# Modulation in quarters, a reordered beginning and weight loads in halves, in a hybrid short-convolution and state-space kernel

## The chip, the cores and the metric

The kernel runs on one core of one Trainium2 chip. The metric is the time of one execution on the device in microseconds (us); lower is better. A profiled execution gives the trace from which the rows below are taken, and its times count from the start of its span.

## The reference

One layer of a streaming encoder is applied to a prompt of 2048 tokens and to a sample of 64 tokens, all in float32 with 1024 channels. Cut to what matters here:

```python
mod = c @ w_mod + b_mod                      # w_mod: 1024 x 3072
shift, scale, gate = jnp.split(mod, 3, axis=-1)
h = rmsnorm(x, norm_in_w) * (1 + scale[:, None]) + shift[:, None]
proj = h @ w_in                              # w_in: 1024 x 7184
b_gate, c_gate, h_a, g_a, z, xbc_raw, dt_raw = jnp.split(proj, idx, axis=-1)
# mixer A: y_a = gated_rmsnorm(b_gate * dwconv3(c_gate * h_a), g_a)
# mixer B: chunked state-space scan over dwconv4 + SiLU of xbc_raw, gated by z
out = jnp.concatenate([y_a, y_b], axis=-1) @ w_out
return rmsnorm(x + gate[:, None] * out, norm_f_w)   # and the new conv and scan states
```

So the input projection needs the normalised x, and the shift and scale of all 1024 channels, which come from a product of the conditioning vectors of prompt and sample with the first 2048 columns of w_mod.

## The kernel before, in words

The kernel is written for a manual schedule: every engine works through its own queue in the order of the program, and an instruction waits until its operands are written and its target is free. Engines are called PE (TensorE), ACT (ScalarE), DVE (VectorE), POOL (GpSimd) and SP (which issues all DMAs).

**The projection** is done transposed: h lies in SBUF as channels by tokens, and the product of 128 output columns with 512 tokens is a matmul of a 128 x 128 weight tile with 128 x 512 of h, summed over channels in a PSUM bank. Each operand is split into a high and a low part (`split`: ACT casts, DVE subtracts), and three matmuls (high-high, high-low, low-high) make one product of float32 quality. The first pass takes 1024 tokens, as two halves of 512. Channels and tokens are halved into four blocks of 4 k-tiles of 128 channels each: A11 and A12 are the two channel halves of tokens 0 to 511, A21 and A22 those of tokens 512 to 1023. The work list holds pairs of two times 128 output columns (`work[g]`). From the third pair on (g = 2) the loop at L1226 forms each pair with seven block products (`PRODS`: A11, S1, S2, S4, S3, A12, A22, where S1 to S4 are sums and differences of the blocks) of 12 matmuls each: a Strassen form. The first two pairs are formed plainly with the four blocks and 8 times 12 matmuls each (`plain_product`, L1041), because their blocks come first; S1 to S4 are made meanwhile (`sum_task`, L1092; split at L1021 and L1028). `plain_w` splits a quarter of a pair's weights (L171, L172), `w_hi` and `w_lo` those of the Strassen pairs, `first_w` those of pair 2 in the beginning.

**The beginning**, whose order is written out by hand: x of tokens 0 to 1023 is loaded as eight row tiles of 128 tokens (`load_rows`). ACT squares each and sums (L979), DVE and POOL make the reciprocal root, DVE scales the rows (`x_scale`). PE transposes them, four row tiles to a bank, one bank per k-tile (`turn_first`), and ACT and DVE in turn copy the banks to the stage tiles stA11 to stA22. Banks come from a rotating list, `ring`.

The shift and scale (**modulation**) are made in two halves (`mod_half`). A half is 4 k-tiles of shift and of scale: 2 times 512 columns of w_mod, loaded as eight pieces of 512 KB, each with 2 k-tiles of w_mod's rows and 512 columns (`load_piece`; eight buffers praw). For each of the 8 k-tiles four products of 32 x 256 go to the four 32-row strips of one bank (L917). ACT copies the result (mrow), PE turns it (L923), DVE adds bias and norm weight, and the columns land in bcol (shift) and scol (scale). `block` then applies them to a stage tile's k-tile, ACT casts it to the high part, DVE subtracts for the low part.

SP's order is: x (eight tiles), pieces of half 0 with the nine small parameter rows between them, the weights of pair 0 (`w_load`: one DMA of 1 MB), pieces of half 1, the weights of pair 1, and so on. PE's order is: transposes of x but for the last four k-tiles, parameter rows, half 0, the last transposes, pair 0 with A11 and A21, half 1, pair 1 with A11, pair 0 with A12 and A22, pair 1 with A21, pair 1 with A12 and A22, and then the loop. `w_load(g + 2)` is called in slot 1 of group g, into the buffer that group g leaves.

After the first pass come the second pass (1088 tokens, read back from DRAM), and the mixing phase with the scan and the output projection; the change doesn't touch their code, other than that `w_load` serves all pairs.

Of the kernel before, what the change touches and what calls it, by code (L numbers as in the profile page):

```python
# [8 lines left out]
F32 = mybir.dt.float32  # L9
F32R = mybir.dt.float32r  # L10
# [17 lines left out]
def kernel(  # L28
# [72 lines left out]
    def phase_project():  # L101
# [78 lines left out]
        raws = [hs1.tile([128, KT, 256], F32, tag=f"raw{i}", name=f"raw{i}") for i in range(2)]  # L180
# [40 lines left out]
        def w_load(g):  # L221
            if g >= len(work):
                return
            raw = raws[g % 2] = hs1.tile([128, KT, 256], F32, tag=f"raw{g % 2}", name="raw")
            col = work[g][0]
            SP.dma_start(out=raw, in_=w_in[:, col:col + 256].rearrange("(k p) f -> p k f", p=128))
            wstate[g] = {"raw": raw, "w": {}}
# [679 lines left out]
        def load_piece(g, j):  # L907
            t = mp.tile([128, 2, 512], F32, tag="praw", name="praw", bufs=8)
            SP.dma_start(out=t, in_=w_mod.rearrange("(p k) n -> p k n", k=KT)[:, 2 * j:2 * j + 2, g * 512:(g + 1) * 512])
            return t  # L910

        def mod_half(half, pieces):
            ps = bank()
            for kk in range(KT):
                for j in range(4):
                    raw = pieces[half + 2 * (j // 2)][kk // 2]
                    PE.matmul(ps[32 * j:32 * j + 32, 0:256], cpad[:, kk, :],  # L917
                              raw[:, kk % 2, 256 * (j % 2):256 * (j % 2) + 256], start=(kk == 0), stop=(kk == KT - 1))
            mrow = mp.tile([128, 256], F32, tag="mrow", name="mrow")
            ACT.copy(out=mrow, in_=ps[:, 0:256])  # L920
            pm = bank()
            for i in range(2):
                PE.transpose(pm[:, i * 128:(i + 1) * 128], mrow[:, i * 128:(i + 1) * 128], ident)  # L923
            m = stats.tile([128, 2, 4, 2], F32, tag="mcol", name="mcol", bufs=1)
            for i in range(2):
                DVE.tensor_copy(out=m[:, :, i::2, :],
                                in_=pm[:, i * 128:(i + 1) * 128].rearrange("p (a b q) -> p a b q", a=2, q=32)[:, :, :, 0:2])
            ks = slice(4 * half, 4 * half + 4)
            for a, col in ((0, bcol), (1, scol)):
                bm = ini[:, 64 + 8 * a + 4 * half:68 + 8 * a + 4 * half].unsqueeze(2).to_broadcast([128, 4, 2])  # L930
# [706 lines left out]
```

## Time and profile before

| | us |
|---|---|
| Median of the runs (lowest, highest) | 1771.92 (1771.90, 1772.29) |
| The profiled execution's own time | 1769.35 |
| Its span | 1767.5 |
| PE busy in the span | 1716.4 (97%) |
| DVE busy | 1306.8 (74%) |
| ACT busy | 826.9 (47%) |
| First plain product (L1041) | starts at 34.51 |
| First product of the loop (L276) | starts at 86.00 |

A row of the timeline has the start, the duration, the engine, the line, the operation, what it writes and reads, how many were merged, and in brackets how long the engine was idle before it and what ended that. PEld is PE's loading of the stationary operand, which overlaps its matmuls. A product of two float32 operands (not split) is recorded as two matmuls. A row of the windows has the stretch, its length, and for each engine the busy time and the number of instructions; then the granted clock of PE as a share of the full one, the busy share of the DMA engines, and GB/s. In the chain in order of time a row is the start, the duration and what the chain passed through.

### The profile page before, as it was taken

The page shows a single profiled execution, that of the slowest core. Times are in us where ns is not written, and L with a number is a line of the kernel's source. Part 1 is how long each engine was busy: PE and PEld are TensorE (multiplying, and loading weights), DVE is VectorE, ACT ScalarE, POOL GpSimd, SP SyncE. Part 2 cuts the span into 40 slices and gives each one's busy share as a digit, 9 for nine tenths or more (in the row PEclk, how much of TensorE's full clock was granted, in tenths as well). Part 3 has the DMA queues.
Part 4 walks back from the last instruction along what each step waited for, and adds up shares of the span by engine and source line. Part 5 has one row for each costly group of instructions (what it writes and reads, how often), then busy time and mean ns, then how long its engine had stood idle before and what let it go on. Part 6 is the DMA issues. An engine that isn't in the chain of part 4 may idle for free.

```text
span 1767.5 us, 26974 instructions
## 1 busy us (share of the span) xinstructions
PE 1716.4 (97%) x10561; PEld 1512.3 (86%) x10561; DVE 1306.8 (74%) x2019; ACT 826.9 (47%) x1575; POOL 102.5 (6%) x224
## 2 busy tenths in 40 slices
PE   5999999999999999999999999999899999999997
PEld 4788888887887799999999999999588888888886
DVE  5787779766576646678768767646788888888885
ACT  5644344444653645434333443325455555545551
POOL 0000000000000000001001000000011111101011
PEclk9999999999999999999999999999899999999999
DMA  9222323232548742322322242324653343434341
GB/s 338 72 76 92 96 84 102 89 107 86 170 151 287 248 123 61 91 74 76 113 82 73 74 119 79 113 90 143 213 179 139 137 150 125 160 107 169 108 149 36
DMA packets 186722, 220.20 MB, mean 125 GB/s; under 512 B 21300, under 2 KB 152356, under 8 KB 186596
## 3 DMA queue, kind: packets, MB, share of 16 engines
q1 hardware_dynamic: 186596, 218.49, 38.2%
q8 instruction: 83, 1.36, 0.3%
q14 instruction: 43, 0.35, 0.1%
HBM read 164.31 MB, written 54.15 MB: 124 GB/s over the span
## 4 chain that ended last, share of the span: by engine, by line
PE 86%; DVE 5%; DMA 4%; ACT 3%; issue 2%; SPq 0%; POOL 0%; POOLq 0%; DVEq 0%; ACTq 0%
PE bank L276 54%; PE mm L1430 14%; PE mm L1437 7%; PE sd L1355 2%; PE sd L1359 2%; PE sd L1361 2%; PE sd L1327 1%; DMA h_q<-hs_d 1%; PE sd L1331 1%; DMA praw<-in_w_mod_dram 1%; PE bank L1041 1%; DVE w L233 1%; DMA hq_d<-h_q 0%; DMA xt<-in_x_prompt_dram 0%; PE bank L530 0%
## 5 line engine op out<-in xcount | busy, mean ns | idle before, releaser
L276 PE MATMUL bank<-hiS,w 128*128 128x272 f32 (+1 forms) x2560 | 598.8, 323 | 9.6 <-ACT keep L301 9.5
L276 PEld LDWEIGHTS bank<-hiS,w 128*128 128x128 f32 x2560 | 432.4, 189 | 46.4 <-ACT keep L301 13.0
L276 PE MATMUL bank<-hiA,w 128*128 128x272 f32 (+1 forms) x1920 | 448.9, 322 | 5.8 <-DVE z_row L309 2.4
L276 PE MATMUL bank<-loS,w 128*128 128x272 f32 (+1 forms) x1280 | 412.4, 322 | 0.0
L276 PEld LDWEIGHTS bank<-hiA,w 128*128 128x128 f32 x1920 | 322.8, 188 | 34.7 <-DVE z_row L309 3.3
L233 DVE TENSOR_TENSOR w<-raw,w 128x512 fp32r<-128x512 f32 x318 | 217.9, 688 | 160.0 <-ACT w L242 149.0
L242 ACT CAST w<-raw 128x512 fp32r<-128x512 f32 x318 | 196.1, 622 | 256.7 <-PE bank L276 131.2
L276 PE MATMUL bank<-loA,w 128*128 128x272 f32 (+1 forms) x960 | 308.2, 321 | 0.0
L276 PEld LDWEIGHTS bank<-loS,w 128*128 128x128 f32 x1280 | 242.2, 189 | 15.8
L276 PEld LDWEIGHTS bank<-loA,w 128*128 128x128 f32 x960 | 180.5, 188 | 11.9
L301 ACT COPY keep<-bank 128x272 f32<-128x272 f32 (+1 forms) x240 | 105.9, 450 | 130.7 <-PE bank L276 130.2
L382 DVE SCALAR_TENSOR_TENSOR acc<-raw_row,par,acc 128x1024 f32<-128x1024 f32 (+1 forms) x96 | 126.5, 1318 | 2.0
L233 DVE TENSOR_TENSOR raw<-raw 128x512 f32<-128x512 f32 x161 | 111.0, 690 | 3.7
L1430 PE MATMUL mm<-woh,vbh 128*128 128x512 f32 (+1 forms) x272 | 110.0, 404 | 0.0
L1430 PE MATMUL mm<-woh,vah 128*128 128x512 f32 (+1 forms) x272 | 109.4, 402 | 0.0
L1430 PE MATMUL mm<-wol,vbh 128*128 128x512 f32 (+1 forms) x272 | 106.6, 392 | 0.0
L1430 PE MATMUL mm<-wol,vah 128*128 128x512 f32 (+1 forms) x272 | 106.4, 391 | 0.0
L1289 ACT ACTIVATE lt<-rb,acum 128x128 f32<-128x128 f32 x240 | 73.4, 388 | 3.5 <-DMA rb<-r_d 3.1
L242 ACT CAST w<-t 128x512 fp32r<-128x512 f32 x53 | 32.8, 618 | 74.1 <-PE bank L276 74.1
L1437 PE MATMUL mm<-woh,vbh 128*128 128x512 f32 (+1 forms) x272 | 67.2, 389 | 0.0
L1437 PE MATMUL mm<-woh,vah 128*128 128x512 f32 (+1 forms) x272 | 67.2, 389 | 0.0
L1455 ACT ACTIVATE t<-xr 128x512 f32<-128x512 f32 (+1 forms) x34 | 21.5, 633 | 92.9 <-DVE xr L1454 92.9
(282 smaller groups left out, 2381.8 us busy)
## 6 DMA issues: line engine op xcount, KB each, us to landing
raw<-in_w_in_dram SPq DMA_DIRECT2D x56, 1024.0 KB
xb_d<-acc SPq DMA_DIRECT2D x32, 512.0 KB
xb<-xb_d SPq DMA_DIRECT2D x32, 512.0 KB
rb<-r_d SPq DMA_DIRECT2D x30, 512.0 KB
xt<-in_x_prompt_dram SPq DMA_DIRECT2D x16, 512.0 KB
praw<-in_w_mod_dram SPq DMA_DIRECT2D x16, 512.0 KB
z_d<-z_row SPq DMA_DIRECT2D x16, 512.0 KB
va_d<-c_row SPq DMA_DIRECT2D x16, 512.0 KB
```

The source lines that it names most:

```text
L233: DVE.tensor_tensor(out=out, in0=a, in1=b, op=ALU.subtract)
L242: ACT.copy(out=w[:, 0], in_=w_src(g, j))
L276: PE.matmul(ps[:, 0:n], w[:, a, k, :], h[:, k, o:o + n], start=(s in (0, 1, 5) and k == 0 and i == 0), stop=(k == 3 and i == 2), skip_grou ...
L301: ACT.copy(out=keep[s][:, o:o + n], in_=b["y" if s == 1 else "x"][:, 0:n])
L382: DVE.scalar_tensor_tensor(out=acc[:, 0:n], in0=r[:, k:k + n], scalar=cb_w(k, t), in1=acc[:, 0:n], op0=ALU.mult, op1=ALU.add)
L1289: ACT.activation(out=lt[:, h, :], in_=rb[:, h, :], func=AF.Relu, scale=-1.0, bias=acum[:, c, h0 + h:h0 + h + 1])
L1355: PE.matmul(py4[64 * e:64 * e + 64, j, :], xd[:, 2 * j + e, :], lt[:, 2 * j + e, :], start=True, stop=True)
L1359: PE.matmul(po4[:, j, :], state[:, hf, j * 128:(j + 1) * 128], xb[:, 6 + j // 2, :], start=True, stop=True)
L1361: PE.matmul(ps[:, g * 256:(g + 1) * 256], bc[:, g, :], xe[:, 4 * g:4 * g + 4, :].rearrange("p h q -> p (h q)"), start=True, stop=True)
L1430: PE.matmul(ps[:n], hl[:, 0, k, 0:n], wo[k0 + k][i][:, nn * 512:(nn + 1) * 512], start=(k == 0 and i == 0), stop=False)
L1437: PE.matmul(ps[:n], hl[:, 1, k, 0:n], wo[k0 + k][0][:, nn * 512:(nn + 1) * 512], start=False, stop=(k == 7))
L1455: ACT.activation(out=t[:n], in_=xr[:n, s], func=AF.Square, accum_out=ss[:n, nn:nn + 1])
```

## The change

- **Modulation in quarters.** A quarter is 2 k-tiles of shift and scale. It needs four pieces of 512 KB, each now 4 k-tiles of w_mod's rows by 256 columns. `mod_half` becomes `mod_mm` (32 products of 32 x 128 to four strips of a bank, and the copy to mrow) and `mod_turn` (one transpose; DVE reads it in PSUM directly, without the copy mcol). The two are called with other work between them for quarters 0 and 1, and directly one behind the other for quarters 2 and 3.
- **Loads.** First x of tokens 0 to 511, quarter 0 with the small rows, half of pair 0's weights (k-tiles 0 to 3), quarter 1, x of tokens 512 to 1023, half of pair 1's weights, the other half of pair 0's; quarter 2, quarter 3, the other half of pair 1's.
- **Order of work.** Pair 0 takes A11's k-tiles 0 and 1 after quarter 0, and 2 and 3 after quarter 1. The squares, the scaling and the transposes of tokens 512 to 1023 come between products. Of a half's four row tiles one is scaled on ACT (`scale_first`). Pair 1 with A11 and pair 0 with A21 come ahead of quarters 2 and 3, and pair 1 with A21 right behind them. S3 is made ahead of quarters 2 and 3, into rows 6 and 7; A21's parts lie in rows 0 to 3.
- **Weights.** `w_load` issues two DMAs of 512 KB for every pair, also in the loop.

```diff
-        def w_load(g):
+        def w_load(g, parts=(0, 1)):
             if g >= len(work):
                 return
-            raw = raws[g % 2] = hs1.tile([128, KT, 256], F32, tag=f"raw{g % 2}", name="raw")
+            if 0 in parts:
+                wstate[g] = {"raw": hs1.tile([128, KT, 256], F32, tag=f"raw{g % 2}", name="raw"), "w": {}}
             col = work[g][0]
-            SP.dma_start(out=raw, in_=w_in[:, col:col + 256].rearrange("(k p) f -> p k f", p=128))
-            wstate[g] = {"raw": raw, "w": {}}
+            for i in parts:
+                SP.dma_start(out=wstate[g]["raw"][:, 4 * i:4 * i + 4, :], in_=w_in[512 * i:512 * i + 512, col:col + 256].rearrange("(k p) f -> p k f", p=128))
...
-        def load_piece(g, j):
-            t = mp.tile([128, 2, 512], F32, tag="praw", name="praw", bufs=8)
-            SP.dma_start(out=t, in_=w_mod.rearrange("(p k) n -> p k n", k=KT)[:, 2 * j:2 * j + 2, g * 512:(g + 1) * 512])
+        def load_piece(q, j):
+            t = mp.tile([128, 4, 256], F32, tag="praw", name="praw", bufs=8)
+            k0, col = 4 * (j // 2), (j % 2) * D + q * 256
+            SP.dma_start(out=t, in_=w_mod.rearrange("(p k) n -> p k n", k=KT)[:, k0:k0 + 4, col:col + 256])
             return t
...
-        def mod_half(half, pieces):
+        def mod_mm(q):
+
             ps = bank()
             for kk in range(KT):
                 for j in range(4):
-                    raw = pieces[half + 2 * (j // 2)][kk // 2]
-                    PE.matmul(ps[32 * j:32 * j + 32, 0:256], cpad[:, kk, :],
-                              raw[:, kk % 2, 256 * (j % 2):256 * (j % 2) + 256], start=(kk == 0), stop=(kk == KT - 1))
-            mrow = mp.tile([128, 256], F32, tag="mrow", name="mrow")
-            ACT.copy(out=mrow, in_=ps[:, 0:256])
+                    raw = pieces[q][2 * (kk // 4) + j // 2]
+                    PE.matmul(ps[32 * j:32 * j + 32, 0:128], cpad[:, kk, :],
+                              raw[:, kk % 4, 128 * (j % 2):128 * (j % 2) + 128], start=(kk == 0), stop=(kk == KT - 1))
+            mrow = mp.tile([128, 128], F32, tag="mrow", name="mrow", bufs=2)
+            ACT.copy(out=mrow, in_=ps[:, 0:128])
+            return mrow
+
+        def mod_turn(q, mrow):
             pm = bank()
-            for i in range(2):
-                PE.transpose(pm[:, i * 128:(i + 1) * 128], mrow[:, i * 128:(i + 1) * 128], ident)
-            m = stats.tile([128, 2, 4, 2], F32, tag="mcol", name="mcol", bufs=1)
-            for i in range(2):
-                DVE.tensor_copy(out=m[:, :, i::2, :],
-                                in_=pm[:, i * 128:(i + 1) * 128].rearrange("p (a b q) -> p a b q", a=2, q=32)[:, :, :, 0:2])
-            ks = slice(4 * half, 4 * half + 4)
+            PE.transpose(pm[:, 0:128], mrow, ident)
+            m = pm[:, 0:128].rearrange("p (a e q) -> p a e q", a=2, q=32)
+            ks = slice(2 * q, 2 * q + 2)
             for a, col in ((0, bcol), (1, scol)):
-                bm = ini[:, 64 + 8 * a + 4 * half:68 + 8 * a + 4 * half].unsqueeze(2).to_broadcast([128, 4, 2])
-                DVE.tensor_tensor(out=col[:, ks, :], in0=m[:, a], in1=bm, op=ALU.add)
-            nin = par[:, 120 + 4 * half:124 + 4 * half].unsqueeze(2).to_broadcast([128, 4, 2])
+                bm = ini[:, 64 + 8 * a + 2 * q:66 + 8 * a + 2 * q].unsqueeze(2).to_broadcast([128, 2, 2])
+                DVE.tensor_tensor(out=col[:, ks, :], in0=m[:, a, :, 0:2], in1=bm, op=ALU.add)
+            nin = par[:, 120 + 2 * q:122 + 2 * q].unsqueeze(2).to_broadcast([128, 2, 2])
...
-        first = [load_rows(range(4), range(4)), load_rows(range(4, 8), range(4, 8))]
+        first = [load_rows(range(4), range(4))]
         load_mods(0)
-        w_load(0)
+        w_load(0, (0,))
+        load_mods(1)
+        first.append(load_rows(range(4, 8), range(4, 8)))
+        w_load(1, (0,))
+        w_load(0, (1,))
...
-        pairs_ss = []
-        for h, xs in enumerate(first):
-            ss = x_ss()
-            for i, (off, n, t) in enumerate(xs):
-                ACT.activation(out=stage["A22"][:, 2 * (i % 2):2 * (i % 2) + 2, :].rearrange("p k t -> p (k t)"), in_=t,
-                               func=AF.Square, accum_out=ss[:, i, 0:1])
-            pairs_ss.append(ss)
-            if h == 0:
-                x_scale(xs, ss, True)
-        turn_first(0, range(4))
-        x_scale(first[1], pairs_ss[1], True)
-        turn_first(0, range(4, 8))
-        turn_first(1, range(4))
+        def square_first(h, i):
+            off, n, t = first[h][i]
+            ACT.activation(out=stage["A22"][:, 2 * (i % 2):2 * (i % 2) + 2, :].rearrange("p k t -> p (k t)"), in_=t,
+                           func=AF.Square, accum_out=first_ss[h][:, i, 0:1])
+
+        def scale_first(h):
+            ms = stats.tile([128, 4], F32, tag="ms4", name="ms4", bufs=2)
+            DVE.tensor_scalar(out=ms, in0=first_ss[h][:, :, 0], scalar1=1.0 / D, scalar2=EPS, op0=ALU.mult, op1=ALU.add)
+            POOL.tensor_tensor(out=ms, in0=ms, in1=mhalf.to_broadcast([128, 4]), op=ALU.pow)
+            for i, (off, n, t) in enumerate(first[h]):
+                if i == 0:
+                    ACT.activation(out=t, in_=t, func=AF.Copy, scale=ms[:, 0:1])
+                else:
+                    DVE.tensor_scalar(out=t, in0=t, scalar1=ms[:, i:i + 1], scalar2=None, op0=ALU.mult)
+
+        first_ss = [x_ss() for _ in range(2)]
+        for i in range(4):
+            square_first(0, i)
+        scale_first(0)
         pt = bank()
         PE.transpose(pt[:, 0:128], rows, ident)
         PE.transpose(pt[:, 128:208], irow, ident[0:80, 0:80])
         DVE.tensor_copy(out=par, in_=pt[:, 0:128])
         DVE.tensor_copy(out=ini, in_=pt[:, 128:208])
+        mrow = mod_mm(0)
+        turn_first(0, range(2))
+        mod_turn(0, mrow)
...
-        mod_half(0, pieces)
-        ring[:] = [4, 5, 6, 7]
-        turn_first(1, range(4, 8))
-        load_mods(1)
-        w_load(1)
         for q in ("A11", "A12", "A22"):
             h_tile(q, 512)
-        rows21 = [[row(4 + 2 * n + i, [128, 2, 512], "a21", F32R) for i in range(2)] for n in range(2)]
         plain_w(0, 0)
-        run([block("A11", k, DVE) for k in range(4)])
+        run([block("A11", k, DVE) for k in range(2)])
         drain()
         plain_w(0, 1)
         for j in range(2):
-            plain_product(0, "A11", j)
+            plain_product(0, "A11", j, range(2))
+        ring[:] = [2, 3, 6, 7]
+        turn_first(0, range(2, 4))
+        mrow = mod_mm(1)
+        turn_first(0, range(4, 6))
+        mod_turn(1, mrow)
+        square_first(1, 0)
+        turn_first(0, range(6, 8))
+        load_mods(2)
+        rows21 = [[row(2 * n + i, [128, 2, 512], "a21", F32R) for i in range(2)] for n in range(2)]
+        run([block("A11", k, DVE) for k in range(2, 4)])
+        drain()
+        for j in range(2):
+            plain_product(0, "A11", j, range(2, 4))
+        for i in range(1, 4):
+            square_first(1, i)
+        plain_w(1, 0)
+        scale_first(1)
+        plain_w(1, 1)
+        plain_product(1, "A11", 0)
+        turn_first(1, range(4))
+        load_mods(3)
+        w_load(1, (1,))
+        plain_product(1, "A11", 1)
         run([block("A21", k, (ACT, DVE)[k % 2]) for k in range(4)])
         drain()
+        turn_first(1, range(4, 8))
         for j in range(2):
             plain_product(0, "A21", j)
+        ring[:] = [6, 7]
         plain_w(0, 2)
         plain_w(0, 3)
         w_load(2)
-        mod_half(1, pieces)
+        S3 = [row(6 + i, [128, 2, 512], "stS3") for i in range(2)]
+        for k in range(4):
+            DVE.tensor_tensor(out=S3[k // 2][:, k % 2, :], in0=stage["A11"][:, k, :], in1=stage["A21"][:, k, :], op=ALU.subtract)
+        for q in (2, 3):
+            mrow = mod_mm(q)
+            mod_turn(q, mrow)
         mods.close()
         for q in ("S1", "S2"):
             home[q] = home.get("S1") or pool(hstack, "hs2", bufs=1, side="right", reuse_waits="tile")
         for q in ("S2", "S1"):
             h_tile(q, 544)
-        plain_w(1, 0)
-        plain_w(1, 1)
-        plain_w(1, 2)
         for j in range(2):
-            plain_product(1, "A11", j)
+            plain_product(1, "A21", j)
+        ring[:] = [4, 5, 6, 7]
         run([block(q, k, (ACT, DVE)[k % 2]) for q in ("A12", "A22") for k in range(4)])
         drain()
         work[0][1]["begin"](0)
         S = [row(2 + i, [128, 2, 512], "stS") for i in range(2)]
...
             if n == 2:
                 drain()
+                plain_w(1, 2)
                 plain_w(1, 3)
                 w_load(3)
...
-        for j in range(2):
-            plain_product(1, "A21", j)
         first_w(1)
         for k in range(4):
             sum_task("S4", k)[0]()
         work[1][1]["begin"](0)
-        S3 = [row(6 + i, [128, 2, 512], "stS3") for i in range(2)]
-        for k in range(4):
-            sum_task("S3", k)[0]()
```

More of the change, by code (lines that the diff above doesn't have):

```diff
@@ L179, in phase_project @@
             row(i, [128, 1094], f"row{i}_")
-        raws = [hs1.tile([128, KT, 256], F32, tag=f"raw{i}", name=f"raw{i}") for i in range(2)]
+        for i in range(2):
+            hs1.tile([128, KT, 256], F32, tag=f"raw{i}", name=f"raw{i}")
         def load_rows(chunks, rows):
@@ L944, in phase_project, with load_mods @@
         small.append((irow[64:80, :], tile_rows(b_mod)[0:16, :]))
-        def load_mods(half):
+        def load_mods(q):
             for j in range(4):
-                for g in (half, half + 2):
-                    pieces[g][j] = load_piece(g, j)
-                    for _ in range(min(2, len(small))):
-                        dst, src = small.pop(0)
-                        SP.dma_start(out=dst, in_=src)
+                pieces[q][j] = load_piece(q, j)
+                for _ in range(min(3, len(small))):
+                    dst, src = small.pop(0)
+                    SP.dma_start(out=dst, in_=src)
         ring[:] = list(range(8))
@@ L1028, in drain, with plain_product @@
                 DVE.tensor_tensor(out=lo, in0=t, in1=hi.bitcast(F32), op=ALU.subtract)
-        def plain_product(g, q, j):
+        def plain_product(g, q, j, ks=range(4)):
             i, f = j // 2, j % 2
             c = 2 * (q in ("A21", "A22")) + f
-            if i == 0:
+            if i == 0 and ks[0] == 0:
                 plain[g]["ps", c] = bank(4 * g + c)
@@ L1037, in plain_product @@
             w = plain[g][j]
-            for k in range(4):
+            for k in ks:
                 hi, lo = (x[k // 2][:, k % 2, :] for x in rows21) if q == "A21" else (x[:, k, :] for x in hq[q])
@@ L1084, in sum_task @@
         def sum_task(q, k):
-            t = (S3 if q == "S3" else S)[k // 2][:, k % 2, :]
+            t = S[k // 2][:, k % 2, :]
             a, b, op = {"S1": (stage["A21"][:, k, :], stage["A22"][:, k, :], ALU.add),
                         "S2": (t, stage["A11"][:, k, :], ALU.subtract),
-                        "S4": (stage["A12"][:, k, :], t, ALU.subtract),
-                        "S3": (stage["A11"][:, k, :], stage["A21"][:, k, :], ALU.subtract)}[q]
+                        "S4": (stage["A12"][:, k, :], t, ALU.subtract)}[q]
             def step():
@@ L1123, in phase_project @@
         work[1][1]["begin"](0)
-        S3 = [row(6 + i, [128, 2, 512], "stS3") for i in range(2)]
-        for k in range(4):
-            sum_task("S3", k)[0]()
         stg_stack.close()
```

## The prediction

> **What bounds the kernel now.** I read the page first (shares of the engines, the chain's shares), then the chain in order of time for the first 110 us, then that stretch's timeline and its windows; the rest of the span only for what the halved weight loads touch. All times are us of the profiled execution.
>
> ```profile
> span 1767.5 us, 26974 instructions
> PE 1716.4 (97%) x10561; PEld 1512.3 (86%) x10561; DVE 1306.8 (74%) x2019; ACT 826.9 (47%) x1575; POOL 102.5 (6%) x224
> PE 86%; DVE 5%; DMA 4%; ACT 3%; issue 2%; SPq 0%; POOL 0%; POOLq 0%; DVEq 0%; ACTq 0%
> ...
> 20.01 7.67 DMA praw<-in_w_mod_dram
> ...
> 34.51 13.12 PE bank L1041 x48
> ...
> 92.51 310.61 PE bank L276 x1368
> ```
>
> TensorE is busy for 97% of the span, and from 92.51 on it runs 311 us without a wait. What the beginning loses before that point is lost for the whole kernel. So the question is one number: when does the steady stretch begin, 92.51 now? Until 27.7 the chain is loads of x and of modulation weights; the first product is at 34.51. What lies between them and 92.51:
>
> ```profile
> 23.74 3.25 PE L917 MATMUL bank<-praw,cpad 128*32 128x256 f32 x52
> ...
> 27.72 1.06 PE L917 MATMUL bank<-praw,cpad 128*32 128x256 f32 x12 [0.74 <-DMA praw<-in_w_mod_dram]
> ...
> 47.56 3.66 PE L917 MATMUL bank<-praw,cpad 128*32 128x256 f32 x64
> ...
> 52.74 0.17 DVE L933 SCALAR_TENSOR_TENSOR scol<-scol,par 128x8 f32<-128x8 f32 x1
> 52.83 1.89 DVE L172 TENSOR_TENSOR w<-raw,w 128x512 fp32r<-128x512 f32 x3
> ...
> 86.00 0.39 PE L276 MATMUL bank<-hiA,w 128*128 128x512 f32 x1
> ...
> 92.51 0.50 PE L276 MATMUL bank<-hiS,w 128*128 128x512 f32 x1 [0.90 <-ACT keep L301]
> 52.20:69.60 17.40, 16.77 (x73) 13.59 (x74) 16.54 (x32) 13.68 (x23) 0.00 (x0) 1.00 0.00 0
> 75.30:95.00 19.70, 18.80 (x83) 15.23 (x83) 16.83 (x28) 12.31 (x23) 0.20 (x2) 1.00 0.23 65
> ```
>
> The last modulation columns (scol) are ready at 52.9. From there two chains run side by side: TensorE's, which reaches the first group of the loop at 86.00, and the one of VectorE and ScalarE (splits of A12, A22, S1 to S4 and the weights), which ends later: the wait before 92.51 is for ScalarE's copy, and the windows show VectorE at 16.54 of 17.40 and 16.83 of 19.70. So **the last modulation plus 39.6 us of vector work (52.9 to 92.5)** sets the start, not the first product.
>
> **The change, part by part.** Durations that the sum uses, all of before:
>
> ```profile
> 15.07 6.58 PE L214 MATMUL bank<-cst,xt 128*128 128x128 f32 x32 [0.19 <-DVE xt L209]
> 29.52 1.91 PE L214 MATMUL bank<-cst,xt 128*128 128x128 f32 x16
> 35.83 1.05 PE L1041 MATMUL bank<-hiA,w 128*128 128x512 f32 x2
> 41.91 5.72 PE L1041 MATMUL bank<-a,w 128*128 128x512 f32 x24
> 11.22 1.02 POOL L207 TENSOR_TENSOR ms<-ms,mhalf 128x4 f32<-128x4 f32 x1 [10.00 <-DVE ms L206]
> 12.28 2.74 DVE L209 TENSOR_SCALAR xt<-xt,ms 128x1024 f32<-128x1024 f32 x4 [1.21 <-POOL ms L207]
> L979 ACT ACTIVATE stA<-xt x8: 1056/1056/1059, 5.9 to 14.8; 128x1024 f32<-128x1024 f32 x8
> 21.85 2.48 DVE L973 COPY stA<-bank 128x512 f32<-128x512 f32 x4
> 38.63 1.17 ACT L1021 CAST a<-stA 128x512 fp32r<-128x512 f32 x2
> 37.78 0.81 ACT L1009 ACTIVATE stA<-stA,bcol,scol 128x512 f32<-128x512 f32 x1
> 41.20 1.29 DVE L1028 TENSOR_TENSOR a<-stA,a 128x512 fp32r<-128x512 f32 x2 [0.17 <-ACT a L1021]
> 51.29 0.37 ACT L920 COPY mrow<-bank 128x256 f32<-128x256 f32 x1 [8.56 <-PE bank L917]
> 80.87 2.49 DVE L1092 TENSOR_TENSOR stS<-stA,stA 128x512 f32<-128x512 f32 x4
> 32.00:33.00 1.00, 0.00 (x0) 0.00 (x0) 0.34 (x1) 0.63 (x2) 0.00 (x0) 1.00 1.05 389
> ```
>
> That gives, in a queue: a product matmul 0.228 (0.43 at half clock), a transpose 0.11 (0.2 in the stretch before 21), a square with its readout 1.28, a 512-wide cast 0.52, a subtraction or evacuation on VectorE 0.60, the scaling of a row 0.66.
>
> *Loads.* The same bytes, in another order: the first quarter (four pieces of 512 KB) stands behind half of x. Before, 8 pieces and all of x landed at 27.7; now 4.2 MB less stand ahead. At the 387 GB/s of the windows below that is 10.8 us less. Pieces with 1 KB rows run a little slower: the weights alone, in such rows, moved 376 and 364, which adds 0.05 to 0.1 a piece. The first quarter is in at 17 to 18, the second at about 25, the last at about 45 (estimates by these rates). The new SP issues are few; SP is nowhere on the chain here.
>
> ```profile
> 35.00:36.00 1.00, 1.00 (x3) 0.67 (x3) 1.00 (x3) 0.32 (x1) 0.00 (x0) 0.50 1.05 387
> 73.00:74.00 1.00, 1.00 (x6) 0.78 (x5) 0.69 (x2) 0.98 (x2) 0.00 (x0) 1.00 1.07 376
> 74.00:75.00 1.00, 1.00 (x6) 0.83 (x5) 0.96 (x3) 0.99 (x2) 0.00 (x0) 1.00 1.06 364
> 1067.61 0.68 PE L711 MATMUL bank<-smp,smp 64*64 64x64 f32 x16
> 1251.57 1.09 PE L1355 MATMUL sd<-lt,xd 128*64 128x128 f32 x16
> ```
>
> *Modulation.* A half was 64 recorded matmuls of 256 columns in 3.66; a quarter is 64 of 128. Half as long each, 1.83, if the columns set the pace; 3.66 if the number does. The nearest rows of narrower matmuls on column tiles: 16 of 64 columns take 0.68, the last one's own 0.22 off: 0.03 each; 16 of 128 columns on two tiles 0.054, which is 0.027 on four. I take 1.83 and keep 3.66 for the range. The Trainium skill has a rule against this edit: its page "TensorE: Matmul & The Clock Gate", section "Wait — 56ns, not 53.3ns?", puts the sequencer at about 62 ns a matmul when its hardware decode is off, which would make a quarter 4.0. The row of 0.03 disagrees.
>
> *The order of the queues.* I walked the five queues in the new order with these durations, each instruction starting when its engine and its operands are free:
>
> 1. First quarter in at 17.4, its remaining matmuls at half clock to 19.4; eight transposes (1.65) to 20.7; transposed row and three short VectorE operations: first scol 21.6.
> 2. Weight subtraction 0.60, block 0.5, cast 0.6: first product at **23.9** (34.5 before). TensorE idled over 3 us, so I take half clock here: 12 products to 28.6 (2.7 at full clock).
> 3. Eight transposes 0.9, second quarter 1.83 (its data long in), eight transposes 0.9: 32.2; second scol 33.0. ScalarE now has an evacuation, a square of the second half of x (1.28) and another evacuation before the cast of A11's third block: cast done 35.3, TensorE idle 2.5. Products to 38.5.
> 4. ScalarE: the cast of the fourth block, three squares 3.84 (35.7 to 39.5), then the weight cast for pair 1: 40.1. TensorE waits 1.9 for it, products to 43.2.
> 5. VectorE is queued behind that weight cast: its subtraction to 40.8, mean 0.2, POOL 1.02, scaling 42.0 to 44.1 (one of four rows now on ScalarE, 1.06, which saves VectorE 0.66 a half). Sixteen transposes 1.8 to 45.6; evacuations to 46.5.
> 6. A21's four blocks: 4.7 (as 37.8 to 42.5 before), to 50.9; the evacuations of x's last quarter behind them (1.2) free bank 2 for A21's products at 51.5. 24 products 5.5: 57.0.
> 7. Only then come quarters three and four, one behind the other: 1.83, copy and transpose 0.6, twice, last scol at **62.5** (61.2 with full clock in step 2). Their data were in 12 us before.
>
> So the second half of x, which in the kernel before is squared, scaled and three quarters turned while loads hold everybody up, now passes through the in-order queues between products, and the last modulation moves from 52.9 to 62.5: 9.6 later. In exchange the vector chain behind it is shorter: S3's four subtractions (2.4) now stand ahead of it, and of three weight subtractions two have gone ahead (1.2): 39.6 - 3.6 = 36.0. The wait in the first loop group ends at 62.5 + 36.0 = 98.5, against 92.5: **+6.0**. TensorE itself reaches that group at about 89.5 instead of 86.0 and then idles about 3.
>
> *Clock.* The rows at 32 to 33 (no TensorE work) and 35 to 36 (clock 0.50) show it halved after an idle stretch of 3 us. The same page, Part 1, has a free-running window of about 3.4 us whose idleness halves the rate; by that rule step 2 and perhaps the wait before 98.5 run at half speed, and where the window falls differs from run to run; the trace agrees. With full clock in step 2 the sum is +4.7; with half clock also after the last wait it is +7.7. I take half clock in step 2 alone.
>
> *Half loads in the loop.* 54 pairs get one more issue.
>
> ```profile
> SPq L226 <- DVE w L233: 267.8, 45, 18.7
> 70.56 0.37 SPq L226 DMA_DIRECT2D raw<-in_w_in_dram  x1
> ```
>
> SP waits for the buffer, not for its own pace, and a group's load is issued a group (84 matmuls of 0.228, 19 us) ahead of its use; the one issued at 70.56 was still moving at 74 to 75 (rows above) and hardly longer. Cost: nothing, with that cover; without it 0.37 per load at one or two places where stores queue behind it (520 to 630), so 0 to +1.
>
> **The sum:** 1767.5 + 6.0 = 1773.5 of span. The execution itself took 1769.35, the median of the runs is 1771.92; against the median: **1778**.
>
> **The rivals.**
> - *TensorE alone sets the start (faster).* From 23.9 on it owes 192 products (43.7), three quarters (5.5), 56 transposes (6.2) and the slow clock (2): 81.3, where 86.0 stood: -4.7, 1767. For it speaks that TensorE was 97% busy and that the data would allow the last modulation at 47.5. It needs the last scol before 92.5 - 36.0 = 56.5; that is the point which decides. Against it: step 6 would have to lose 6 us of waits.
> - *No change beyond 3.5 us.* Full clock throughout and a middle that overlaps 1 to 2 us better than my queues: +1 to +3.5, 1774.
> - *Small matmuls cost by number.* At 0.057 each, a quarter 3.66: +1.8 four times, +13, 1785; against it the 0.03 above. This is where the page's 62 ns would end.
> - *The change doesn't do what it says:* if the first weight split waits for the whole pair's weights, the first product stays at 35, and everything behind it comes 11 later than forecast: +17, 1789. Against such a coarse wait speaks that TensorE began on A11's first block before the fourth was cast:
>
> ```profile
> 34.51 0.73 PE L1041 MATMUL bank<-hiA,w 128*128 128x512 f32 x1 [3.08 <-ACT hiA L1021]
> 36.74 0.62 ACT L1021 CAST hiA<-stA 128x512 fp32r<-128x512 f32 x1 [0.44 <-DVE stA L1011]
> ```
>
>
> **How the numbers follow.** Within 0.2% (3.5 us) a measurement of this kernel can't tell from no change. Forecast (+3.5 to +10): 0.64. TensorE alone: 0.12. No change: 0.14. By number 0.05, coarse wait 0.05. Slower 0.74, same 0.14, faster 0.12. The likeliest case's own range is 1775.5 to 1782 (clock and loop terms, -1 for the walk). To leave out no more than two in ten the range takes in the no-change case and half of the faster one's distance below, and the by-number case above: 1770.5 to 1785.
>
> **What would show it.** First product near 24; 64 recorded modulation matmuls in 1.8; TensorE idle 2 to 3 us before A11's third block, 2 before pair 1, 1.5 before A21; the last scol at 61 to 63, 9 us after the last modulation piece has landed 12 us earlier; at the first loop group a wait for ScalarE's copy three times as long as the 0.90 now; everything behind shifted alike. A last scol before 57 makes the forecast wrong, and so does a vector chain behind it that is not near 36.

## The result, and the profile after

Slower, by more than forecast: 1789.41 us median (1788.56 to 1791.19) against 1771.91, ratio 1.01 with a 95% interval of 1.0084 to 1.0116. That is +17.5 where +6 was forecast; the direction was right, and the time lies above the range. It is close to the 1789 of the rival with the coarse wait, but by chance: that rival had the first product at 35, and it came at 25.35.

The page of the changed kernel, and five pieces of its chain in order of time (start, length, what, matmuls in a row):

```profile
span 1786.4 us, 27300 instructions
PE 1726.6 (97%) x10689; PEld 1516.3 (85%) x10689; DVE 1306.6 (73%) x2019; ACT 828.7 (46%) x1579; POOL 101.8 (6%) x224
PE 84%; DVE 5%; ACT 4%; DMA 4%; issue 2%; SPq 0%; POOL 0%; POOLq 0%; DVEq 0%; ACTq 0%
```

```profile
13.12 3.51 DMA irow<-in_b_mod_dram
17.13 3.57 PE bank L921 x64
25.35 4.75 PE bank L1056 x12
52.35 5.81 PE bank L1056 x24
101.69 316.02 PE bank L278 x1368
```

TensorE's share is the same 97%, and its busy time is 10.2 us longer (the 128 matmuls more are the modulation's, each half as long). The steady stretch starts at 101.69 (92.51 before), and its first 1368 matmuls take 316.02 (310.61). The rest, from 417.71 to the end, takes 1368.7; before, from 403.12, it took 1364.4. So the span's 18.9 us are 9.2 of a later start, 5.4 in that stretch, and 4.3 behind it.

The start. Timeline rows of TensorE (lines 921, 1056, 278) and VectorE (936, the last step of scol; 994, the scaling of x's second half); in brackets the idle time and what ended it:

```profile
17.06 3.64 PE L921 MATMUL bank<-praw,cpad 128*32 128x128 f32 x64
22.73 0.16 DVE L936 SCALAR_TENSOR_TENSOR scol<-scol,par 128x4 f32<-128x4 f32 x1
25.35 0.80 PE L1056 MATMUL bank<-hiA,w 128*128 128x512 f32 x1 [2.92 <-ACT hiA L1036]
30.90 1.96 PE L921 MATMUL bank<-praw,cpad 128*32 128x128 f32 x64
34.34 0.16 DVE L936 SCALAR_TENSOR_TENSOR scol<-scol,par 128x4 f32<-128x4 f32 x1
36.59 0.50 PE L1056 MATMUL bank<-hiA,w 128*128 128x512 f32 x1 [1.71 <-ACT hiA L1036]
40.09 0.60 ACT L171 CAST w<-raw 128x512 fp32r<-128x512 f32 x1
42.63 2.08 DVE L994 TENSOR_SCALAR xt<-xt,ms 128x1024 f32<-128x1024 f32 x3 [1.13 <-POOL ms L989]
52.35 5.81 PE L1056 MATMUL bank<-a,w 128*128 128x512 f32 x24 [1.44 <-ACT w L171]
63.66 0.16 DVE L936 SCALAR_TENSOR_TENSOR scol<-scol,par 128x4 f32<-128x4 f32 x1
90.94 0.39 PE L278 MATMUL bank<-hiA,w 128*128 128x512 f32 x1
101.69 0.80 PE L278 MATMUL bank<-hiS,w 128*128 128x512 f32 x1 [5.10 <-ACT keep L303]
```

The first product came forward from 34.5 to 25.35, and a quarter took 1.96 (the first one 3.64). But the last scol was ready at 63.8 instead of 52.9, and the wait for ScalarE's copy in the first loop group grew from 0.90 to 5.10. Behind it the clock was halved, in the windows' column behind POOL:

```profile
102.00:103.00 1.00, 1.00 (x3) 0.81 (x3) 0.81 (x2) 0.64 (x2) 0.00 (x0) 0.50 0.06 4
106.00:107.00 1.00, 1.00 (x4) 0.71 (x4) 0.24 (x1) 0.00 (x0) 0.00 (x0) 0.50 0.38 118
107.00:108.00 1.00, 1.00 (x5) 0.86 (x4) 0.00 (x0) 0.78 (x2) 0.00 (x0) 0.89 0.00 0
```

Neither explains the later matmuls. The prediction wanted "everything behind shifted alike"; but with the clock full again a loop matmul follows the one before it after 228.9 ns on average, before after 226.9 (starts in the trace, 512 columns).

### The profile page after: what moved, and what is told of

Same layout as the page of the kernel before. It is cut to its first block, busy times and chain, and to the rows that moved or that the text cites. A ratio compares the mean times of both kernels' runs of the same rounds, so it can differ in the third digit from the quotient of the medians.

```text
span 1786.4 us, 27300 instructions
## 1 busy us (share of the span) xinstructions
PE 1726.6 (97%) x10689; PEld 1516.3 (85%) x10689; DVE 1306.6 (73%) x2019; ACT 828.7 (46%) x1579; POOL 101.8 (6%) x224
## 4 chain that ended last, share of the span: by engine, by line
PE 84%; DVE 5%; ACT 4%; DMA 4%; issue 2%; SPq 0%; POOL 0%; POOLq 0%; DVEq 0%; ACTq 0%
PE bank L278 54%; PE mm L1462 13%; PE mm L1469 6%; PE sd L1391 2%; PE sd L1387 2%; PE sd L1393 2%; DMA h_q<-hs_d 1%; DMA wo_raw<-in_w_out_dram 1%; PE sd L1359 1%; PE sd L1363 1%; DVE w L235 1%; PE bank L1056 1%; PE bank L921 1%; ACT w L244 0%; PE bank L532 0%
## 5 line engine op out<-in xcount | busy, mean ns | idle before, releaser
L278 PE MATMUL bank<-hiS,w 128*128 128x272 f32 (+1 forms) x2560 | 603.3, 325 | 13.3 <-ACT keep L303 13.2
```

The lines of the kernel that those rows point to most:

```text
L278: PE.matmul(ps[:, 0:n], w[:, a, k, :], h[:, k, o:o + n], start=(s in (0, 1, 5) and k == 0 and i == 0), stop=(k == 3 and i == 2), skip_grou ...
```

## Experiments on the pace of the matmuls

The change takes one thing away that no step of the prediction looked at: the tile mcol, 64 bytes of each partition in the stats pool. Everything that is allocated behind it moves down by 64 bytes, the loop's weight tiles among it: the compiled program places w0 at byte 31008 instead of 31072. The moving tiles, at the other end of SBUF, stay. (The end with the low addresses is called the left side below.) Rival reasons were the halved loads in the loop, and the chance of one execution.

**The 64 bytes put back** in the changed kernel:

```diff
 ks = slice(2 * q, 2 * q + 2)
+stats.tile([128, 2, 4, 2], F32, tag="mcol", name="mcol", bufs=1)
```

> The changed kernel with a 64-byte tile that nothing reads put back into the stats pool where before had mcol, so that the weight tiles of the loop (w0 at 31072 bytes, as before, not 31008) lie where they lay before. Address theory (the place of the weight tiles sets the pace of the loop's matmuls): mean distance of loop matmuls in the first pass back from 228.9 to 226.7 ns, the drift of about 7 us behind the first groups gone, about 1782.5. Half-load theory (two 512 KB loads per pair instead of one of 1 MB disturb TensorE) and chance-of-the-execution theory: no change, 1788 to 1791, distance 228.9 ns.

Measured: 1782.09 (1781.38 to 1783.98), 7.3 less than the change; against before 1.0063 (1.0051 to 1.0076). The mean distance is back at 226.9 ns. Its chain still has the late start, and a short stretch at half clock:

```profile
101.57 312.20 PE bank L278 x1368
```

**The 64 bytes taken away** from the kernel before (mcol from the pool mp):

```diff
-m = stats.tile([128, 2, 4, 2], F32, tag="mcol", name="mcol", bufs=1)
+m = mp.tile([128, 2, 4, 2], F32, tag="mcol", name="mcol", bufs=1)
```

> The kernel before with mcol's 64 bytes taken from the pool mp instead of stats, nothing else: the weight tiles lie 64 bytes lower, as in the changed kernel. Address theory: distance of loop matmuls in the first pass 228.9 instead of 226.7 ns and about 1778 to 1779 (before: 1772). The other theories: 1772, distance 226.7 ns.

Measured: 1777.65, ratio 1.0043 (1.0031 to 1.0056): +6.4 with not one instruction changed. Its chain:

```profile
92.55 313.47 PE bank L276 x1368
```

Same start as before to 0.04 us, 229.1 ns a matmul instead of 227.1 (310.61 / 1368).

**Whole loads again** in the changed kernel (one transfer of 1 MB from the third pair on):

```diff
+if g >= 2:
+    SP.dma_start(out=wstate[g]["raw"], in_=w_in[:, col:col + 256].rearrange("(k p) f -> p k f", p=128))
+    return
 for i in parts:
```

> The changed kernel with the weights of every pair from the third on loaded by one transfer of 1 MB again; the halves remain for the first two pairs. Half-load theory: the drift of about 7 us goes, about 1782, distance of loop matmuls 226.7 ns. Address theory: no change, 1788 to 1791, 228.9 ns.

Measured: 1790.22 (1786.62 to 1795.69), mean distance 229.0 ns. The pace, which that theory was to change, stayed, so it falls; a cost of the halved loads below a few us can't be seen beside this spread.

**Which tiles, and which places.** Eight more copies of the kernel before, each with one unused tile more (or mcol moved) and nothing else changed. First other amounts in the stats pool:

> The kernel before with 32 bytes more in the stats pool: the weight tiles start 32 bytes higher (w0 at 31104, a multiple of 128 minus 0, instead of 31072). If what counts is whether a tile starts at 96 bytes or 32 bytes past a multiple of 128 because the moving tiles start at 96 (equal offsets are good), the pace gets slower than 226.7 ns and the time rises by 3 to 8 us, 1775 to 1780. If the multiple itself counts (start on a 128-byte line is good): 226.7 ns or less, at most 1772.

> The kernel before with 32 bytes less in the stats pool (w0 at 31040, 64 bytes past a multiple of 128; before 96 past it with 226.9 ns a matmul, the changed kernel 32 past with 228.9, and 0 past with 233.3 and 1792.8 us). Theory that the place within 128 bytes decides and 96 is the one good place: 228 to 234 ns, 1776 to 1793. Theory that only a start on a 64-byte line or the like is bad: 233 ns, 1793. If neither, 226.9 ns and 1771.

> The kernel before with 128 bytes more in the stats pool (w0 at 31200, 96 past a multiple of 128 as before). Theory that the place within 128 bytes decides: 226.9 ns and 1771, no change. Theory that the absolute address, or the distance of the weights to the moving tiles, decides: another pace, 228 to 234 ns, and 5 to 22 us more.

> The kernel before with 256 bytes more in the stats pool. Theory of a period of 256 bytes in the distance of weights to moving tiles: 226.9 ns and 1771. Theory of no period so short: 228 to 234 ns, 1776 to 1793, as with 128 bytes (232.5 ns, 1790.5).

> The kernel before with 64 bytes more in the stats pool. Theory that odd multiples of 32 bytes are the bad ones (233.3 ns at -32 and 32) and even ones mild (228.9 at -64): about 229 ns and 1777. Theory that every other place is as bad as 32: 233 ns, 1790.

| left side moved by (bytes) | us, median | ratio (95%) | chain: length, matmuls | ns each |
|---|---|---|---|---|
| 0 (before) | 1771 | 1 | 310.61, 1368 | 227.1 |
| -64 | 1777.65 | 1.0043 (1.0031 to 1.0056) | 313.47, 1368 | 229.1 |
| -32 | 1793.07 | 1.0128 (1.0107 to 1.0149) | 325.04, 1392 | 233.5 |
| 32 | 1792.80 | 1.0121 (1.0104 to 1.0138) | 325.05, 1392 | 233.5 |
| 64 | 1792.66 | 1.0113 (1.0096 to 1.013) | 319.47, 1368 | 233.5 |
| 128 | 1790.53 | 1.0109 (1.0092 to 1.0126) | 318.17, 1368 | 232.6 |
| 256 | 1771.05 | 0.9999 (0.9989 to 1.0008) | 310.61, 1368 | 227.1 |

My first rules (a place within 128 bytes, a start on some line) fell with 32, 64 and 128. What 256 bytes more leave is exactly what was there before:

```profile
92.34 310.61 PE bank L276 x1368
```

Then only t3 and the kept sums, then the weights and what lies behind them:

> The kernel before with a 32-byte tile in the pool lp between the weight tiles and t3: only t3, the kept sums and junk lie 32 bytes higher; weights, rows and moving tiles stay. Theory that the weights' place sets the pace: 226.9 ns and 1771. Theory that the places of the kept sums or t3 do (ScalarE and VectorE write there while TensorE runs): 228 to 234 ns, 1776 to 1793.

> The kernel before with the 32-byte tile in lp ahead of the weight tiles: w0 to w6 and what lies behind them 32 bytes higher; the rows, the carries and everything of the later phases stay. Theory that the weights' place sets the pace: 233.3 ns as in the run with 32 bytes more in the stats pool, and 13 us more from the loop alone, about 1785 (that run had 1792.8, 8 us of it behind the loop, where other tiles had moved too). Theory of the rows: 226.9 ns and 1771.

The first: 1771.37, ratio 0.9998 (0.9989 to 1.0008). The second: 1784.23, 1.0062 (1.0046 to 1.0078), and

```profile
88.80 325.03 PE bank L276 x1392
```

233.5 ns, as with the whole side moved. So it is the weights. The 8.6 us between 1784.23 and 1792.8 are of later phases, whose tiles moved only in the other run. The traces tell which: the output projection. Its loaded tiles vah and vbh lie on the left side, its moving tiles (woh, wol) do not. One of its groups of 256 matmuls (busy time, mean ns of one, which overlaps the next), first with only the weights of the loop moved, then with the whole side moved by 32:

```profile
L1438 PE MATMUL mm<-woh,vah 128*128 128x512 f32 x256 | 63.2, 389 | 0.0
```

```profile
L1438 PE MATMUL mm<-woh,vah 128*128 128x512 f32 x256 | 64.9, 395 | 0.0
```

On average its matmuls follow each other after 227.6 and 233.1 ns, which makes about 9 us over its 1632 matmuls of 512 columns; from the first product of the mixing phase to the end the two runs took 523.4 and 531.8.

Last, the weights left alone, and the hi and lo tiles of the four sums moved down by 32 bytes:

> The kernel before with a 32-byte tile in the pool of the moving tiles, by which the hi and lo tiles of the four sums lie 32 bytes lower; those of the blocks and all weights stay. Theory that the distance of the weights to the moving tiles sets the pace: the products with sums (four of seven) at another distance, 228 to 234 ns, those with blocks 226.9 as before; 4 to 9 us more. Theory that the weights' own place sets it: 226.9 ns for all and 1771.

Measured: 1778.94, ratio 1.0035 (1.0025 to 1.0046). One loop group of its timeline:

```profile
148.32 0.40 PE L277 MATMUL bank<-hiS,w 128*128 128x512 f32 x1
...
159.52 0.39 PE L277 MATMUL bank<-hiA,w 128*128 128x512 f32 x1
...
167.70 0.40 PE L277 MATMUL bank<-hiS,w 128*128 128x512 f32 x1
```

From 148.32 to 159.52 run 48 matmuls with sums, 233.3 ns each; from 159.52 to 167.70 run 36 with blocks, 227.2 each. Same weights, same group, same clock: so the place of the weights alone does not decide. In the kernel before, the starts lie 94720 (hi of S1) and 146944 bytes (hi of A11) from w0, both multiples of 256. These runs, which move one of the two tiles and never both, leave one other reading: that each has a good place of its own, since in the loop of the kernel before both start 96 bytes past a multiple of 256. The output projection of the same kernel speaks against it: there both start 224 bytes past a multiple of 256, and a matmul takes 227.5 ns as well. So **the distance of the weight tile to the moving tile decides**, not the place of either. Which distances between these multiples are how bad, five shifts show but no rule explains.

## Experiments on the beginning

With the 64 bytes back, 10.8 us over before remain (1782.09 to 1771.25). The forecast had "last modulation plus vector chain" for this part. These runs, all but the first on top of the 64 bytes (the next two names stand for them), test it.

**Quarters three and four ahead of A21's products**, in the changed kernel as it was:

```diff
+for q in (2, 3):
+    mrow = mod_mm(q)
+    mod_turn(q, mrow)
 for j in range(2):
     plain_product(0, "A21", j)
```

> The changed kernel with the products and transposes of the third and fourth quarter of the modulation moved ahead of A21's products of pair 0 (the data have landed by then, TensorE waits there 1.4 us for A21's blocks). Theory that the last scol and VectorE's and ScalarE's chain behind it set when the first loop group's second product can start: last scol at about 55 instead of 63.8, the wait in the first loop group ends at 93 to 95 instead of 101.7, no stretch of half clock behind it, 8 to 11 us less, about 1780. Rival, the chain is held by TensorE's products and the casts of weights ahead of it and not by the last scol: less than 3 us.

Measured: 1788.20 (1786.19 to 1791.33), 1.2 less, which is within the spread. A miss: I had not counted the bank. TensorE waited for VectorE's copy of a transpose, ran the quarters slower (the clock was halved from 55.6 to 59.0), and the last scol came only 2.4 earlier:

```profile
54.40 2.60 PE L921 MATMUL bank<-praw,cpad 128*32 128x128 f32 x64 [1.94 <-DVE stA L979]
61.30 0.16 DVE L936 SCALAR_TENSOR_TENSOR scol<-scol,par 128x4 f32<-128x4 f32 x1
102.95 0.50 PE L278 MATMUL bank<-hiS,w 128*128 128x512 f32 x1 [3.35 <-ACT keep L303]
```

And the wait ended 41.5 behind that scol, not 37.9 (this execution was 1.5 late before the quarters already): a first sign that "scol plus a fixed chain" is not a law.

**The quarters spread** among the products, ahead of x's second half:

```diff
 plain_w(1, 0)
+mrow = mod_mm(2)
 scale_first(1)
 plain_w(1, 1)
+mrow3 = mod_mm(3)
 turn_first(1, range(4))
+mod_turn(2, mrow)
+mod_turn(3, mrow3)
```

> Start: the changed kernel with the 64-byte filler (1782.1). In it the products of the third quarter go behind the third and fourth blocks' products of A11 and those of the fourth quarter right behind them, both ahead of the transposes of x's second half, and pair 1's products with A11 follow the transposes; all loads of quarters are issued in one place. Theory (last scol, then the chain of VectorE and ScalarE): last scol at 47 to 49 instead of 63.6; the chain is then held by what stands ahead of A12's blocks (A21's blocks, the copies of the transposes, two weight pieces, S3's subtractions), and these blocks start at 57 to 58 instead of 62.8: the wait in the first loop group ends 5 to 6 us earlier, at about 96, TensorE's idle time there falls from 5.2 to 1 to 2 us and the half clock behind it goes (2.6 more): about 1774. Rival, the chain is held by TensorE's products and not by scol: under 3 us.

Measured: 1783.39 (1779.6 to 1784.61), no gain over the 64 bytes alone.

```profile
46.45 1.07 PE L921 MATMUL bank<-praw,cpad 128*32 128x128 f32 x28 [0.95 <-DMA praw<-in_w_mod_dram]
50.21 0.16 DVE L937 SCALAR_TENSOR_TENSOR scol<-scol,par 128x4 f32<-128x4 f32 x1
61.67 0.54 DVE L1027 TENSOR_SCALAR stA<-stA,scol,bcol 128x512 f32<-128x512 f32 x1
99.64 0.79 PE L278 MATMUL bank<-hiS,w 128*128 128x512 f32 x1 [4.44 <-ACT keep L303]
```

The last scol came 13.3 us earlier (50.4 for 63.7), the wait ended 1.9 earlier (101.57 with the 64 bytes), and that in the fastest of the four executions. A12's blocks, which need that scol, start on VectorE only at 61.67: A21's blocks, copies, two weight pieces and S3's subtractions stand ahead of them. So the last scol alone did not hold the chain; what stood ahead in the same queues, most of it work on the second half of x, did so as much.

**S3's subtractions back** behind S4's, as before:

> The changed kernel with the filler (1782.1), and S3's four subtractions back behind S4's, where before had them. The prediction's step: they lie on the path there, 2.4 us more, about 1784.5. Theory of the two traces: ScalarE's queue sets this stretch (its casts start when S4's subtractions are done), and VectorE has 1.46 us of idle time behind them; 2.4 less 1.46 gives 0.9 to 1.0 more, about 1783.

Measured: 1783.37 (1782.4 to 1786.13), +1.3; the wait ends at 102.93, 1.4 later. But the last scol was 0.8 late already (the second one as well, so this came ahead of S3's old and new place). The last scol and the wait, with the 64 bytes alone and then with S3 back:

```profile
63.55 0.16 DVE L937 SCALAR_TENSOR_TENSOR scol<-scol,par 128x4 f32<-128x4 f32 x1
101.57 0.72 PE L278 MATMUL bank<-hiS,w 128*128 128x512 f32 x1 [5.24 <-ACT keep L303]
```

```profile
64.37 0.16 DVE L937 SCALAR_TENSOR_TENSOR scol<-scol,par 128x4 f32<-128x4 f32 x1
102.93 0.79 PE L278 MATMUL bank<-hiS,w 128*128 128x512 f32 x1 [5.76 <-ACT keep L303]
```

Behind the last scol, S3's subtractions cost 0.5 (38.4 for 37.9): less than the queues' 0.9 to 1.0, and far less than the prediction's 2.4. Why the 2.4 did not come, rows of ScalarE and VectorE show, the changed kernel first, then before:

```profile
88.17 2.49 DVE L1128 TENSOR_TENSOR stS<-stA,stS 128x512 f32<-128x512 f32 x4
90.69 1.14 ACT L1036 CAST hiS<-stS 128x512 fp32r<-128x512 f32 x2 [3.77 <-DVE stS L1128]
```

```profile
80.99 1.14 ACT L1021 CAST hiS<-stS 128x512 fp32r<-128x512 f32 x2 [3.77 <-DVE stS L1092]
```

In both, ScalarE idles 3.77 until S4's last subtraction and is dense behind it. S3's four came behind that point, beside ScalarE's work.

**S4's subtractions ahead** of the second loop weights:

```diff
 first_w(0)
+for k in range(4):
+    sum_task("S4", k)[0]()
```

> The changed kernel with the filler (1782.1), and S4's four subtractions right behind the first loop weights' hi and lo instead of behind the second ones. Theory that ScalarE idles 3.8 us for them and its dense queue behind sets the wait in the first loop group: the first cast of hiS4 3.0 us earlier (87.5), VectorE fills its idle 1.8 us, the wait ends 1.8 to 3 us earlier, about 1779 to 1780.5. Rival, TensorE or the loads hold it: no change.

Measured: 1779.32 (1777.74 to 1781.64), -2.8. The profiled execution, the slowest of the four, had reached the loop 0.9 late and gained 1.3 from there; a new wait took the rest, ScalarE's copy into a row that the store of z_row still reads:

```profile
91.16 0.59 ACT L1061 COPY c_row<-bank 128x512 f32<-128x512 f32 x1 [1.65 <-DMA z_d<-z_row]
101.12 0.80 PE L278 MATMUL bank<-hiS,w 128*128 128x512 f32 x1 [3.89 <-ACT keep L303]
```

**x's second half early as well.** ScalarE idled from 25.1 to 30.9 while its pieces landed:

```diff
     plain_product(0, "A11", j, range(2))
+for i in range(4):
+    square_first(1, i)
...
 mrow = mod_mm(1)
+scale_first(1)
...
+turn_first(1, range(4))
 for j in range(2):
     plain_product(0, "A11", j, range(2, 4))
...
 plain_product(1, "A11", 0)
 turn_first(1, range(4, 8))
+mrow = mod_mm(2)
+mrow3 = mod_mm(3)
+mod_turn(2, mrow)
+mod_turn(3, mrow3)
```

> Start: the changed kernel with the 64-byte filler (1782.1). The squares of x's second half stand behind the first products (ScalarE idles there from 25.1 to 30.9), its scaling behind the second quarter's products, its first four transposes ahead of A11's third block's products; the third and fourth quarters' products follow pair 1's first product with A11. Theory: in the changed kernel the later start of x's second half (scaled at 42.6, A21's blocks done at 51.6) holds VectorE's and ScalarE's chain as much as the last scol does, which is why the quarters alone gave 1.9. Here scaling at 31 to 34, A21's blocks done at 44 to 46, last scol at 49 to 52, A12's blocks from 50 to 53; the wait in the first loop group ends near 90 (101.6 with the filler alone) or is gone, no half clock behind it: 11 to 13 us less, 1769 to 1771. Rival, transfers hold these steps: less than 4 us.

Measured: 1775.62 (1774.01 to 1777.32), 6.5 less than with the 64 bytes alone, about half of what I expected.

```profile
63.81 1.29 DVE L1129 TENSOR_TENSOR stS<-stA,stA 128x512 f32<-128x512 f32 x2 [2.93 <-PE bank L1056]
96.06 0.50 PE L278 MATMUL bank<-hiS,w 128*128 128x512 f32 x1 [3.42 <-ACT keep L303]
```

The wait ends 5.5 earlier. Early quarters alone had moved it by 1.9: x's second half, with A21's blocks and S3's subtractions, which this run moved up with it, was the other bound. The order of some loads changed too, and no run moved x's second half without the quarters, so what each part gives by itself is not shown. The chain now runs into TensorE.

**Both together**, the last one's order and S4 ahead:

> The kernel of the run before this one, and S4's subtractions ahead of the second loop weights. If the wait in the first loop group is still there after the earlier squares, 1 to 2 us less than without; if TensorE alone sets the start by then, the same within 0.5 us.

Measured: 1773.06 (1771.04 to 1776.45), ratio 1.0012 (1.0003 to 1.0021), 2.6 less. The wait is down to 2.07:

```profile
93.94 0.50 PE L278 MATMUL bank<-hiS,w 128*128 128x512 f32 x1 [2.07 <-ACT keep L303]
```

All but 1.6 of the 17.5 us are back, with the early first product and the halved loads kept.

**S in other rows**, so that VectorE does not wait for A21's products:

```diff
-S = [row(2 + i, [128, 2, 512], "stS") for i in range(2)]
+S = [row(4 + i, [128, 2, 512], "stS") for i in range(2)]
```

> The kernel with earlier squares and S4's subtractions ahead (1773.1), and the sums S in rows 4 and 5 instead of 2 and 3, which A21's hi and lo hold until pair 1's products with A21 are done (VectorE waited 2.9 us for them). Theory that the chain of VectorE and ScalarE still sets the wait of 2.1 us in the first loop group: the wait and the half clock behind it go, 2 to 4 us less, 1769 to 1771. Rival, TensorE's products set it: no change.

Measured: 1773.40, ratio 1.001 (1.0001 to 1.0019): no change, the rival holds. ScalarE now waits at the next place for TensorE:

```profile
67.22 0.59 ACT L1060 COPY z_row<-bank 128x512 f32<-128x512 f32 x1 [5.48 <-PE bank L1056]
93.74 0.50 PE L278 MATMUL bank<-hiS,w 128*128 128x512 f32 x1 [2.08 <-ACT keep L303]
```

No order that I ran beats the kernel before.

## Why the prediction was wrong, step by step

| step | forecast | measured |
|---|---|---|
| 1 first scol | 21.6 | 22.9 |
| 2 first product; 12 products at half clock | 23.9; 4.7 | 25.35; 4.75 |
| 3 second scol, third block's products | 33.0, 35.3 | 34.5, 36.59 |
| 4, 5 pair 1's cast, scaling | 40.1, 42.0 | 40.7, 42.63 |
| 6 A21's products | 51.5 | 52.35 |
| 7 last scol | 62.5 | 63.8 |
| vector chain behind it | 36.0 | 37.9 |
| wait in the first loop group ends | 98.5 | 101.69 |
| half clock behind that wait | not taken (+1.7) | about 2.6 |
| all matmuls behind | shifted alike | 7.2 more |

The order of the queues was right: each step came 0.6 to 1.5 late, the last scol 1.3, as the first scol already. That delay arose in step 1: TensorE waited until 16.8 for a small parameter row (irow), and then all 64 matmuls of the first quarter ran slowly, to 20.7, where the prediction had only the remaining ones slow, to 19.4. The small matmuls cost by columns (1.96 a quarter; 3.66 would have been by number), the coarse wait did not come, and TensorE alone did not set the start. The halved loads cost nothing that shows, as forecast.

Three terms failed. The largest is "everything behind shifted alike": the removed tile moved the weights by 64 bytes, and the loop's matmuls ran at 228.9 instead of 226.9 ns. No step of the prediction asked whether the weights stay where they lay. Putting the 64 bytes back gave 7.3 us: the time of 1782.1 then lies inside the forecast range, though the cost is still 10.8 where 6.0 was forecast. The second is the chain: "S3's four subtractions (2.4) now stand ahead of it" counted VectorE's time alone, where ScalarE's queue behind S4 set the pace; measured behind the last scol, it was 0.5. The difference of 1.9 is all by which the chain was forecast too short; it rests on one execution of each kernel. The third is the clock: I kept half clock behind the last wait as an alternative and did not take it, though I forecast that TensorE would idle 3 us there. It idled 5.1, and the stretch of 1368 matmuls took 316.02 where the kernel before, with its weights at the same distance, took 313.47.

Together 1.3 + 1.9 + 2.6 + 7.2 make 13.0 beside the forecast 6.0, the span's 18.9 within rounding.

Beside these, a reading of the profile was too simple. "The last modulation plus 39.6 us of vector work sets the start" held as a sum in both kernels (39.6 and 37.9), but not as a cause: with the last scol 13.3 earlier the start moved 1.9. Both inputs of the queues, the scol and the work on x's second half, had become late, and moving the scol only uncovered the other.

## What to carry to other kernels

A tile that goes or comes moves everything allocated behind it. Compare the addresses of TensorE's two operands before and after an edit, and keep their distance (here a multiple of 256 bytes); a run of the old kernel with the old size restored, or an unused tile added, separates this from what the edit is about. When a wait is put down to one late input, ask which other inputs of the same in-order queue arrive in its shadow, before counting its removal as a gain.

## What the runs showed of the hardware

*Weights and moving data.* A matmul of 512 columns took 227.1 to 233.5 ns by the distance of its weight tile to its moving tile, in programs that were otherwise the same; 256 bytes more gave the first value back. With 272 columns, in the second pass, it hardly shows: 125.3 ns before, 125.6 with the weights 32 bytes higher. The Trainium skill's page "SBUF — State Buffer", section "A bandwidth-pool intuition that's wrong (but worth ruling out)", gives the weight load a second, independent read port, and its section "SBUF: two separate sides" has TensorE never wait on anyone. If that is read to mean that the place of one operand can't slow the reading of the other, the run in which only the sums' tiles moved disagrees: 233.3 ns with them, 227.2 with the blocks, in one loop group. The measurement decides; where the two reads meet, no run here shows.

*The clock after a short wait.* Two of the runs had the same wait, 2.07 and 2.08 us. In one the clock was then halved, in the other not (windows of the run with both together, and of the one with S in other rows):

```profile
96.00:97.00 1.00, 1.00 (x3) 0.73 (x3) 0.47 (x1) 0.45 (x1) 0.00 (x0) 0.50 1.02 354
```

```profile
96.00:97.00 1.00, 1.00 (x6) 0.84 (x5) 0.26 (x2) 0.65 (x2) 0.00 (x0) 1.00 1.07 376
```

The Trainium skill's page "TensorE: Matmul & The Clock Gate", Part 1, has a free-running window of about 3.4 us, so that the point of change depends on where work falls in it; these two runs agree. But the same part asks for at least one idle window, and 2.07 us is less than one: a wait of 2 us can be enough.

The traces also show when it is enough. In all twenty of them the granted clock changes only on a grid of 3.41 us. In the first of the two runs the whole wait, 91.87 to 93.94, lies in one step of that grid, 91.68 to 95.09, and the clock was halved from 95.09 to 98.50. In the second, whose clock changed at 24.33 and 31.16, a point of the grid lies at 92.6 and cuts the wait, 91.66 to 93.74, into 0.9 and 1.1. Over all twenty traces, 9971 steps at full clock had less than 1.6 us without a matmul, and the clock stayed full behind every one; 123 had 1.95 us or more, and it was halved behind every one; the 34 between went both ways.
